# A state scan between projections on one Trainium2 core: a step's small matmuls in two bunches, its transfers merged, Tm copied behind R

## The chip, the cores and the metric

One core of a Trainium2 chip runs the whole program. The metric is the device time of one execution in microseconds; of the kernel before three runs are known. A profile shows one execution. TensorE (PE) multiplies matrices and adds up in PSUM; VectorE (DVE) and ScalarE (ACT) work on tiles in SBUF and PSUM; GpSimd (POOL) does little here; SyncE (SP) issues all transfers from one queue, in order. Every engine works through its own instructions in order.

## The reference, cut to what matters

Two sequences of 512 tokens and 1024 channels (s = 0 and 1) go through two layers. Layer 0 is RWKV-7 time mixing in both directions, 16 heads of 64 channels; its scan is

```
S_t = S_{t-1} (diag(decay_t) + a_t b_t^T) + v_t k_t^T ;  y_t = S_t r_t
```

with r, k, v and a gate z from 1024 x 1024 projections of the shifted input, a group norm behind it, and an output projection w_o. Layer 1 is attention over a neighbourhood of 8 x 16 grid cells, with one input projection (q, k, v, z) and one output projection. All is float32 at the interface; the projections run as three passes of a rounded form (high by high, high by low, low by high).

## The kernel before, in words

The kernel has three stages. A prelude (to about 165 us) norms the inputs and computes z and k of s = 0. The scan phase (about 167 to 1146 us, the last step ends there) is the stage that the change touches. The rest is attention and the remaining projections.

The scan is cut into chunks of 64 tokens. `self.todo` lists 8 pairs (s, pb), each of four heads, and each pair has 8 steps (chunks; both directions are in one step), so there are 64 steps q. For a pair `prep` computes the factors of the chunks and stores them (dram `ab`), `gram` their products, and `inverse` inverts a triangular matrix by 30 elimination steps on VectorE (the tiles N and etmp) and 32 x 32 matmuls. The result is MT. `finish` norms the outputs of a pair.

A step works so, by the names of the code:

- `fetch` loads `cab` (the chunk's factors, two transfers, one per direction) and `V` (four transfers); `fetch_x` loads the other half of `X` (two transfers) from the same dram tile `vt`.
- `near` (L979): 8 matmuls A K^T into a spare part of the bank `zy` of the step before, then VectorE masks them into `AK`.
- `outer` (L1000): 32 matmuls into the tile `pf` (one buffer, shared with `gram`); VectorE masks the first half into `R` (L1024), ScalarE copies the second half into `Tm` (L1031).
- `step` (L1035): `S` times `cab` and `V` times `AK` into `zy` (L1061, L1067); ScalarE copies `Z` (L1073); the solve, MT times Z, into `us` (L1083); ScalarE copies its halves into `X` (L1087); the next state, X times Tm, into `us` (L1093); then the outputs, X times R, into `zy` (L1098); VectorE makes `WS` and `S` (L1107, L1108) and the outputs are copied or added into `y` (L1113, L1115).

Next to it `flow` runs the projections: `loads` brings raw weights, `splits` makes the high half `whi` on ScalarE (L687) and the low half `wlo` on VectorE (L689), `operands` does the same with a column group's inputs (loaded into `xr`, two buffers; copied to `act` at L710 and L712), `products` issues three passes for each of 8 blocks k of a column (L727 to L729), and `posts` runs `column`, which takes the finished column out of its bank `pm`.

What sets the order: in the scan phase the order on TensorE, VectorE and ScalarE is written out by a planner at build time, `weave`. Each of the functions above is a thread; it yields the engine that its next piece needs, a condition (`gate`) and an estimate of when its data is there. `weave` keeps a model clock per engine, and takes, of the threads that are open and ready, the one of the lowest rank, those of TensorE last. Thus `step` (rank 0) goes before `near` (0.5), `outer` (1), `operands` (3.5) and `products` (9), and products fill what is left. `room` and `left` of `Clock` estimate when a bank or buffer is free. On the chip each engine keeps the order that was planned, and waits where a semaphore is late. Outside the scan phase the framework's scheduler sets the order.

In `step` each `yield` is a point at which other work can come between:

```
1089         yield "P", lambda: did["R"] > q and did["X"] > q, lambda c: c.at(name(st.X, st.R[0], *([] if st.last else st.Tm[:1])))
...
1094             yield "P"
```

Of the kernel before, what the change touches and what calls it, by code (L numbers as in the profile page):

```python
# [10 lines left out]
F32 = mybir.dt.float32  # L11
# [38 lines left out]
class Clock:  # L50
# [7 lines left out]
    def __init__(self, nc):  # L58
        self.nc = nc
        self.t = dict.fromkeys("PADGS", 0.0)  # L60
        self.made, self.used = {}, {}
        self.slots = {}
        self.slot = {}
        self.dq = 0.0
        self.mode, self.tiles = None, {}
        self.seen = 0
# [146 lines left out]
class Trunk:  # L213
    NACT, NW, NRAW, NTMP, WP = 18, 4, 3, 5, 512
# [18 lines left out]
    NZ1, STOCK, EPS = 0, 1, 60.0  # L233
# [338 lines left out]
    def shifted(self, s, j):  # L572
        xn, xx = self.shift[s]

        def source(k):
            t = self.t("xr", bufs=2)
# [5 lines left out]
    def reload(self, kind, s):  # L582
        return self.operands(lambda k: self.load(self.t("xr", bufs=2), self.sp[kind, s, k]))


    def column(self, s, kind, p, ps):
# [3 lines left out]
        first = lambda e: (e, None, lambda c, n=ps.tensor.name: c.at([n]))  # L590
        if kind == "z":
# [6 lines left out]
            yield "A" if s == 0 else first("A")  # L598
            act.activation(th, ps, AF.Tanh, scale=0.5)
            yield "D"  # L600
            vt.scalar_tensor_tensor(o, th, 1.0, ps, op0=ALU.add, op1=ALU.mult)
# [3 lines left out]
        o = self.tmp()  # L605
        act.copy(o, ps)
# [4 lines left out]
        if kind == "k":  # L611
            yield "A"
            sq = self.tmp()
# [25 lines left out]
        if p == 0:  # L639
            sp["vt", s] = self.dram(f"vt{s}", (NCH, 4, 2, L, 2, P))  # L640
# [3 lines left out]
        for d in range(2):  # L644
# [8 lines left out]
            for j in range(2):  # L653
                self.load(sp["vt", s][j::2, p // 2, d, :, p % 2].rearrange("m t c -> t m c"), vs[64 * j:64 * j + 64])
# [10 lines left out]
    def flow(self):  # L665
# [5 lines left out]
        raw, w, x = {}, {}, {}  # L671
# [20 lines left out]

        def operands():
            for g, (ready, source, _) in enumerate(self.groups):
                if g == 0:
                    continue
                todo = []
                for k in range(KT + 1):
                    if k < KT:
                        yield "S", lambda: ready() and 8 * g + k < did["x"] + self.NACT // 2 + 1  # L700
                        todo.append(source(k))
                    if k == 0:
                        continue
                    src, before = todo.pop(0)
                    for n, f in enumerate(before):
                        yield "D", None, lambda c: c.at(name(src))
                        f()
                    yield "A", lambda: 8 * g + k - 1 < did["x"] + self.NACT // 2, lambda c: c.at(name(src))
# [4 lines left out]
                    x[g, k - 1] = hi, lo  # L713
# [21 lines left out]
        def posts(a):  # L735
# [7 lines left out]
            Thread(lambda: 0, loads()), Thread(lambda: 3 if few() else 9, splits()), Thread(lambda: 3.5, operands()),  # L743
# [215 lines left out]
    def fetch(self, st):  # L959
# [6 lines left out]
        for d in range(2):  # L966
            self.load(st.ab[:, d].rearrange("p g a t -> p g (a t)"), sp["ab", s, pb][i][:, d])
        for d in range(2):
            for h in range(2):
                self.load(st.V[half(h), d], sp["vt", s][i, pb, d][:, :, 64 * h:64 * h + 64])  # L970

    def fetch_x(self, st):
        sp, s, pb, i, e = self.sp, st.s, st.pb, st.i, st.e
        half = lambda h: slice(64 * h, 64 * h + 64)
        st.X = self.t("X", (P, 2, 2, 2, HD), self.NX, F32, self.front)
        for d in range(2):
            self.load(st.X[half(1 - e[d]), d].rearrange("p g h v -> p (g h v)"), sp["vt", s][i, pb, d].rearrange("t g c -> t (g c)"))

    def near(self, q):  # L979
# [3 lines left out]
        free, room = self.bank()  # L983
        yield (
            "P", lambda: self.did["fetch"] > q and (self.did["solve"] >= q if q else free()),
# [774 lines left out]
```

## Time and profile before

| what | us |
|---|---|
| median of 3 runs | 1789.09 |
| lowest and highest run | 1788.36, 1797.47 |
| the profiled execution | 1786.57 |
| its span, first to last instruction | 1784.6 |
| TensorE busy | 1602.6 (90%) |
| VectorE busy | 1238.0 (69%) |
| ScalarE busy | 978.6 (55%) |
| mean granted clock of TensorE | 0.962 |

The page's shares are over the whole span. The stages differ: behind the scan phase TensorE is always busy, in it it is not. In a row of a timeline the first number is the start, the second the duration, and a bracket at the end is the idle time of the engine before it, with what ended it. The granted clock is a share of 2.4 GHz: 1.0 is that, 0.5 is 1.2 GHz, and a value between is a mixture over the stretch. Matmuls overlap: two that follow each other start closer together than one lasts.

### The profile page before, as it was taken

The numbers are of one execution on the slowest core, as the hardware profiler recorded it, in microseconds if no ns is written. First come the engines' busy times: TensorE is split into PE (matmuls) and PEld (weight loads), VectorE is DVE, ScalarE is ACT, GpSimd is POOL, SyncE is SP. The second block draws the span as 40 slices with busy tenths as digits, with TensorE's granted clock in tenths as the row PEclk, the third lists the DMA queues.
The fourth block names the chain that finished last, engine by engine and source line by source line (L and its number), as shares of the span: only waits on it lengthen the run. The fifth ranks groups of instructions, "written<-read, shape, count | busy, mean of one in ns | idle before, by whom it ended". The sixth has DMA issues, their size and how long they took to land.

```text
span 1784.6 us, 49663 instructions
## 1 busy us (share of the span) xinstructions
PE 1602.6 (90%) x20416; PEld 1231.1 (69%) x20416; DVE 1238.0 (69%) x2693; ACT 978.6 (55%) x1964; POOL 24.2 (1%) x94
## 2 busy tenths in 40 slices
PE   7997767889889888798898977999999999999998
PEld 6775546666556666676675766788777788777776
DVE  8977578877878778886787966532556676655564
ACT  5454456667484575666557443333556665545562
POOL 0000000000000000000000000000000000000000
PEclk9999888999999999999998989999999999999999
DMA  5435667577666577767765775564546346644452
GB/s 197 160 130 199 201 222 220 179 224 212 199 195 204 185 228 219 239 197 228 215 198 187 239 218 159 158 236 149 171 159 198 105 135 219 207 158 148 166 183 95
DMA packets 252675, 336.49 MB, mean 189 GB/s; under 512 B 57280, under 2 KB 122944, under 8 KB 252448
## 3 DMA queue, kind: packets, MB, share of 16 engines
q1 hardware_dynamic: 252448, 333.32, 58.1%
q8 instruction: 160, 2.62, 0.6%
q14 instruction: 67, 0.55, 0.1%
HBM read 227.71 MB, written 105.51 MB: 187 GB/s over the span
## 4 chain that ended last, share of the span: by engine, by line
PE 58%; DVE 18%; DMA 10%; ACT 7%; issue 5%; SPq 1%; DVEq 0%; ACTq 0%
PE pg L403 6%; PE pg L404 6%; PE pg L405 6%; PE pm L727 5%; PE pm L728 4%; PE pm L729 4%; DMA cab<-dab 3%; PE pm L1316 3%; DVE etmp L917 2%; PE po L1344 2%; DVE N L918 2%; PE pt L1331 2%; DVE ab L840 2%; PE pf L1016 2%; SPq L308 1%
## 5 line engine op out<-in xcount | busy, mean ns | idle before, releaser
L727 PE MATMUL pm<-act,whi 128*128 128x512 f32 x608 | 271.5, 447 | 33.7 <-ACT whi L687 18.3
L729 PE MATMUL pm<-act,wlo 128*128 128x512 f32 x608 | 247.2, 407 | 6.4 <-DVE wlo L689 6.3
L728 PE MATMUL pm<-act,whi 128*128 128x512 f32 x608 | 248.0, 408 | 5.5 <-DVE act L712 5.4
L403 PE MATMUL pg<-act,whi 128*128 128x512 f32 x448 | 182.1, 408 | 0.2 <-DVE tmp L1274 0.2
L404 PE MATMUL pg<-act,whi 128*128 128x512 f32 x448 | 178.2, 398 | 0.0
L405 PE MATMUL pg<-act,wlo 128*128 128x512 f32 x448 | 177.8, 397 | 0.0
L353 DVE TENSOR_TENSOR wlo<-raw,whi 128x512 fp32r<-128x512 f32 x156 | 107.1, 688 | 91.5 <-ACT whi L352 76.0
L727 PEld LDWEIGHTS pm<-act,whi 128*128 128x128 f32 x608 | 118.4, 195 | 71.3 <-ACT whi L687 20.4
L352 ACT CAST whi<-raw 128x512 fp32r<-128x512 f32 x156 | 96.3, 618 | 126.2 <-PE pg L404 61.6
L689 DVE TENSOR_TENSOR wlo<-raw,whi 128x512 fp32r<-128x512 f32 x152 | 103.7, 686 | 74.6 <-ACT whi L687 74.4
L729 PEld LDWEIGHTS pm<-act,wlo 128*128 128x128 f32 x608 | 119.3, 196 | 36.7 <-DVE wlo L689 10.5
L728 PEld LDWEIGHTS pm<-act,whi 128*128 128x128 f32 x608 | 119.5, 197 | 31.8 <-DVE act L712 9.4
L687 ACT CAST whi<-raw 128x512 fp32r<-128x512 f32 x152 | 93.8, 620 | 66.2 <-PE pm L728 50.8
L403 PEld LDWEIGHTS pg<-act,whi 128*128 128x128 f32 x448 | 84.4, 188 | 25.5 <-issue 10.4
L405 PEld LDWEIGHTS pg<-act,wlo 128*128 128x128 f32 x448 | 84.3, 188 | 17.9 <-issue 1.7
L404 PEld LDWEIGHTS pg<-act,whi 128*128 128x128 f32 x448 | 84.4, 188 | 17.5 <-issue 2.7
L918 DVE TENSOR_TENSOR N<-etmp,N 128x30 f32<-128x30 f32 (+14 forms) x240 | 79.8, 332 | 8.2
L1327 ACT ACTIVATE sb<-sb,mx 128x256 f32<-128x256 f32 x128 | 64.1, 503 | 36.6 <-DVE mx L1326 36.1
L1031 ACT COPY Tm<-pf 128x512 f32<-128x512 f32 x56 | 32.8, 586 | 92.2 <-DVE R L1024 92.0
L917 DVE TENSOR_TENSOR etmp<-N 128x30 f32<-128x30 f32 (+14 forms) x240 | 78.7, 328 | 5.0
L1016 PE MATMUL pf<-cab 64*64 64x64 f32 x2048 | 51.1, 234 | 29.7 <-DMA cab<-dab 21.4
L1324 DVE CUSTOM_DVE_ANT_0 sb<-pm,bias 128x256 f32<-128x256 f32 x128 | 50.0, 420 | 39.2 <-PE pm L1316 30.2
(370 smaller groups left out, 3424.2 us busy)
## 6 DMA issues: line engine op xcount, KB each, us to landing
dab<-ab SPq DMA_DIRECT2D x32, 1024.0 KB
cab<-dab SPq DMA_DIRECT2D x128, 256.0 KB
raw<-in_w_in_dram SPq DMA_DIRECT2D x128, 256.0 KB
bias<-in_rpb_dram SPq DMA_DIRECT2D x32, 384.0 KB
raw<-in_w_z_dram SPq DMA_DIRECT2D x32, 256.0 KB
dz<-tmp SPq DMA_DIRECT2D x32, 256.0 KB
raw<-in_w_k_dram SPq DMA_DIRECT2D x32, 256.0 KB
dk<-tmp SPq DMA_DIRECT2D x32, 256.0 KB
```

Source lines behind the costliest of these rows:

```text
L352: self.nc.scalar.copy(hi, src)
L353: (eng or self.nc.vector).tensor_tensor(lo, src, hi.bitcast(F32), op=ALU.subtract)
L403: nc.tensor.matmul(ps, hi, x[k][0], start=(k == 0), stop=False)
L404: nc.tensor.matmul(ps, hi, x[k][1], start=False, stop=False)
L405: nc.tensor.matmul(ps, lo, x[k][0], start=False, stop=(k == KT - 1))
L687: nc.scalar.copy(hi, raw[h])
L689: nc.vector.tensor_tensor(lo, raw.pop(h), hi.bitcast(F32), op=ALU.subtract)
L727: nc.tensor.matmul(ps, hi[:, at], xh, start=(k == 0), stop=False)
L728: nc.tensor.matmul(ps, hi[:, at], xl, start=False, stop=False)
L729: nc.tensor.matmul(ps, lo[:, at], xh, start=False, stop=(k == KT - 1))
L917: vt.tensor_tensor(tv, N[:, q + 1:, q:q + 1].broadcast_to([P, n, q]), N[:, q:q + 1, :q].broadcast_to([P, n, q]), op=ALU.mult)
L918: vt.tensor_tensor(N[:, q + 1:, :q], tv, N[:, q + 1:, :q], op=ALU.add)
```

## The change

It does seven things.

1. `near` and `outer` lose their matmuls. A new function `factors(q + 1)` issues both, 8 and 32, directly behind the solve of step q in the same piece of TensorE's order. The solve is issued only when `factors` can be (next `cab` loaded, `pf` free) or when the next step starts a pair. `alone` issues `factors` where no solve before did.
2. Next state and outputs are one piece: the `yield "P"` between them goes. It may be planned 400 ns (`NEAR`) before its inputs are there.
3. `Tm` is copied when `R` is made, by the planner's estimate, and not before step q - 1 is through (`did["steps"] >= q`).
4. `vt` is laid out so that `V` is one transfer, `X` still two; its store has rows of 256 bytes instead of 512. `cab` is one transfer.
5. `xr` has three buffers (`NXR`). A thread `fetched` of rank 0 loads operands; `operands` has rank 2.5.
6. Banks that a column of k or z, or the outer products, will read a second time are noted in `keep`, so that the planner does not count them as free.
7. The index order of `X` and `us` is (h, g) instead of (g, h).

```diff
     def left(self, name):
-        return max(self.used.get(name, {}).values(), default=0.0) if name in self.slot else 1e12
+        return max(self.used.get(name, {}).values(), default=0.0) if name in self.slot and name not in self.keep else 1e12
...
         if p == 0:
-            sp["vt", s] = self.dram(f"vt{s}", (NCH, 4, 2, L, 2, P))
+            sp["vt", s] = self.dram(f"vt{s}", (4, 2, NCH // 2, 2, L, 2, 2, HD))
...
+        def fetched():
+            for g, (ready, source, _) in enumerate(self.groups):
+                for k in range(KT if g else 0):
+                    yield "S", lambda: ready() and 8 * g + k < did["x"] + self.NACT // 2 + self.NXR - 1
+                    todo[g, k] = source(k)
...
-        for d in range(2):
-            self.load(st.ab[:, d].rearrange("p g a t -> p g (a t)"), sp["ab", s, pb][i][:, d])
-        for d in range(2):
-            for h in range(2):
-                self.load(st.V[half(h), d], sp["vt", s][i, pb, d][:, :, 64 * h:64 * h + 64])
+        self.load(st.ab.rearrange("p d g a t -> p (d g a t)"), sp["ab", s, pb][i].rearrange("p d g a -> p (d g a)"))
+        self.load(st.V.rearrange("p d g c -> p (d g c)"), sp["vt", s][pb, i % 2, i // 2].rearrange("h t d g c -> (h t) (d g c)"))
...
+    def factors(self, q):
...
+        st.ak = self.steps[q - 1].room if q else self.p("pm", (P, 2, 2, L))
         for g in range(2):
             for dd in range(2):
                 for h in range(2):
                     nc.tensor.matmul(
-                        ak[half(h), dd, g], ab[half(h), dd, g, 1 + e[dd]], ab[half(h), dd, g, 2 - e[dd]], start=not q, stop=True,
+                        st.ak[half(h), dd, g], ab[half(h), dd, g, 1 + e[dd]], ab[half(h), dd, g, 2 - e[dd]], start=not q, stop=True,
                         skip_group_check=True)
...
+        self.clock.keep.add(st.f.tensor.name)
+        self.did["factors"] += 1
...
-            yield "A", None, lambda c: c.at([f.tensor.name])
+            yield "A", lambda: did["steps"] >= q, lambda c: c.at([R.tensor.name])
...
-        yield "P", lambda: did["inverse"] > st.n and free2(), lambda c: max(c.at(name(Z, self.formed[key][1])), room2(c))
+        near, wide = self.bank("pf")
+        go = lambda: q + 1 < len(self.steps) and did["factors"] == q + 1 and did["fetch"] > q + 1 and near()
+        yield (
+            "P", lambda: did["inverse"] > st.n and free2() and (go() or not self.soon(q + 1)),
+            lambda c: max(c.at(name(Z, self.formed[key][1])), room2(c), max(c.at(name(self.steps[q + 1].ab)), wide(c)) if go() else 0.0))
...
         did["solve"] += 1
+        if go():
+            self.factors(q + 1)
...
-        yield "P", lambda: did["R"] > q and did["X"] > q, lambda c: c.at(name(st.X, st.R[0], *([] if st.last else st.Tm[:1])))
+        yield (
+            "P", lambda: did["R"] > q and did["X"] > q,
+            lambda c: c.at(name(st.X, st.R[0], *([] if st.last else st.Tm[:1]))) - self.NEAR)
...
-            yield "P"
```

Three places show what the planner makes of it. On TensorE, one step in the middle of the phase, before (X is what ScalarE copied from the solve, h and w2h belong to `prep`):

```order
L1061 MATMUL zy_10762<-S_10745,cab_10018 64x64 x16
L1067 MATMUL zy_10762<-V_10019,AK_10701 64x64 x8
L1016 MATMUL pf_10799<-cab_10274 64x64 x16
L1016 MATMUL pf_10799<-cc,cab_10274 64x64 x16
L1083 MATMUL us_10838<-Z_10832,MT_439_1696 64x64 x8
L993 MATMUL zy_10762<-cab_10274 64x64 x8
L796 MATMUL pm_10860<-h_1407_7574,w2h_10663 128x512
L797 MATMUL pm_10860<-h_1407_7574,w2l_10662 128x512
L1093 MATMUL us_10838<-X_10224,Tm_10238 64x64 x8
L796 MATMUL pm_10880<-h_1430_7767,w2h_10663 128x512
L797 MATMUL pm_10880<-h_1430_7767,w2l_10662 128x512
L1098 MATMUL zy_10762<-X_10224,R_10236 64x64 x8
```

and of the changed kernel, a step near it (L1105 is the solve, L1119 the next state, L1123 the outputs):

```order
L1105 MATMUL us_10710<-Z_10702,MT_439_1696 64x64 x8
L998 MATMUL zy_10659<-cab_10187 64x64 x8
L1008 MATMUL pf_10727<-cab_10187 64x64 x16
L1008 MATMUL pf_10727<-cc,cab_10187 64x64 x16
L736 MATMUL pm_10455<-act_8519,whi_10461 128x512
L737 MATMUL pm_10455<-act_8518,whi_10461 128x512
L738 MATMUL pm_10455<-act_8519,wlo_10462 128x512
L1119 MATMUL us_10710<-X_10293,Tm_10688 64x64 x8
L1123 MATMUL zy_10659<-X_10293,R_10656 64x64 x8
L736 MATMUL pm_10455<-act_8533,whi_10461 128x512
L737 MATMUL pm_10455<-act_8532,whi_10461 128x512
L738 MATMUL pm_10455<-act_8533,wlo_10462 128x512
```

The outer products moved from before the solve to behind it, and the outputs moved up to the next state. On ScalarE, around the copies of a step, before:

```order
L1073 COPY Z_10989<-zy_10911 128x256
L1031 COPY Tm_11000<-pf_10956 128x512
L652 COPY vs_11012<-pm_10993 128x512
L1087 COPY X_10758<-us_11002 64x256 x2
L852 ACTIVATE pp_11033<-th_1924_10897,dv 128x512
L652 COPY vs_11040<-pm_11027 128x512
```

and of the changed kernel:

```order
L1111 COPY X_10908<-us_10998 64x256 x2
L809 ACTIVATE th_1979_11090<-pm_11063,dv 128x512
L813 ACTIVATE u_11092<-th_1979_11090,ones 128x512
L1138 COPY y_10177<-zy_10957 128x256
L1048 COPY Tm_11104<-pf_11015 128x512
L809 ACTIVATE th_1988_11140<-pm_11094,dv 128x512
L660 COPY vs_11142<-pm_11099 128x512
L1091 COPY Z_11181<-zy_11108 128x256
```

Tm stood between Z and X of a step; now it stands behind X and y, and ahead of the next step's Z. On VectorE, around the update of a state, before (ab, kp belong to `prep`, etmp and N to `inverse`):

```order
L1024 TENSOR_TENSOR R_10998<-pf_10956,mrx_1693 128x512
L840 TENSOR_TENSOR ab_10953<-pp_10954,u_10950 128x4x2x64
L997 TENSOR_TENSOR AK_11016<-zy_10911,cc 128x256
L917 TENSOR_TENSOR etmp_10651<-N_10649 128x210
L918 TENSOR_TENSOR N_10649<-etmp_10651,N_10649 128x10x21
L689 TENSOR_TENSOR wlo_10688<-raw_10481,whi_10687 128x512
L855 TENSOR_TENSOR kp_1946_11055<-pp_11033,k_10656 128x512
L840 TENSOR_TENSOR ab_10953<-kp_1946_11055,u_10950 128x4x2x64
L1107 TENSOR_TENSOR WS_11074<-us_11002,S_10893 128x256
L1108 TENSOR_TENSOR S_11073<-WS_11074,wc_7484 128x256
```

and of the changed kernel:

```order
L1031 TENSOR_TENSOR AK_11051<-zy_10957,cc 128x256
L864 TENSOR_TENSOR kp_1973_11055<-pp_11053,k_10627 128x512
L849 TENSOR_TENSOR ab_10931<-kp_1973_11055,u_10928 128x4x2x64
L1041 TENSOR_TENSOR R_11068<-pf_11015,mrx_1693 128x512
L1132 TENSOR_TENSOR WS_11087<-us_10998,S_10949 128x256
L1133 TENSOR_TENSOR S_11086<-WS_11087,wc_7020 128x256
L1188 TENSOR_TENSOR bv_10695<-pm_10919,bv_10695 128x512
```

The work of the other threads that stood between R and WS moved ahead of R or behind S.

## Rows read from the trace of the kernel before

**Rows 1.** The page's head and its count of transfer packets.

```profile
span 1784.6 us, 49663 instructions
...
DMA packets 252675, 336.49 MB, mean 189 GB/s; under 512 B 57280, under 2 KB 122944, under 8 KB 252448
```

**Rows 2.** Busy time by stage: PE, PEld, DVE, ACT, POOL, clock, DMA share, GB/s.

```profile
170.00:305.00 135.00, 92.67 (x913) 69.82 (x915) 97.30 (x171) 73.12 (x137) 6.20 (x11) 0.86 0.65 212
305.00:1146.00 841.00, 724.36 (x15594) 552.64 (x15589) 649.06 (x1244) 493.62 (x977) 16.11 (x39) 0.95 0.66 205
1146.00:1785.00 639.00, 630.04 (x3288) 490.45 (x3286) 351.92 (x1018) 329.13 (x711) 0.00 (x0) 1.00 0.50 166
```

**Rows 3.** TensorE's waits, 170 to 1146: total us, times, longest us.

```profile
PE pf L1016 <- DMA cab<-dab: 21.4, 19, 4.2
PE pm L727 <- ACT whi L687: 18.3, 4, 14.3
PE pm L727 <- ACT act L710: 11.4, 5, 7.1
PE us L1083 <- ACT Z L1073: 9.9, 12, 1.7
...
PE pf L1016 <- ACT Tm L1031: 8.2, 3, 3.6
...
PE pm L729 <- DVE wlo L689: 6.3, 8, 1.5
PE us L1093 <- ACT X L1087: 6.1, 7, 2.1
...
PE zy L1061 <- DVE S L1108: 3.9, 4, 2.3
```

**Rows 4.** Timeline of TensorE around one lone next-state group, full clock.

```profile
901.09 0.39 PE L728 MATMUL pm<-act,whi 128*128 128x512 f32 x1
901.32 0.40 PE L729 MATMUL pm<-act,wlo 128*128 128x512 f32 x1
901.65 0.69 PE L1093 MATMUL us<-X,Tm 128*64 128x64 f32 x16
902.26 0.50 PE L796 MATMUL pm<-h,w2h 128*128 128x512 f32 x1
902.60 0.40 PE L797 MATMUL pm<-h,w2l 128*128 128x512 f32 x1
```

**Rows 5.** The same around a solve with A K^T directly behind it.

```profile
851.36 0.40 PE L729 MATMUL pm<-act,wlo 128*128 128x512 f32 x1
851.69 0.68 PE L1083 MATMUL us<-Z,MT 64*64 64x64 f32 x16
852.20 0.63 PE L993 MATMUL zy<-cab 64*64 64x64 f32 x16
852.77 0.50 PE L796 MATMUL pm<-h,w2h 128*128 128x512 f32 x1
```

**Rows 6.** SP's issues of cab and V: ns min/median/max, first and last start.

```profile
L308 SPq DMA_DIRECT2D cab<-dab x128: 319/430/2650, 242.3 to 1127.4; - x128
...
L308 SPq DMA_DIRECT2D V<-dvt x256: 512/597/2153, 291.0 to 1129.8; - x128
```

**Rows 7.** The tiles R, WS, Tm: durations, and ScalarE's idle time before Tm.

```profile
L1024 DVE TENSOR_TENSOR R<-pf,mrx x64: 642/684/693, 300.6 to 1135.1; 128x512 f32<-128x512 f32 x64
...
L1107 DVE TENSOR_TENSOR WS<-us,S x48: 386/418/446, 342.7 to 1138.9; 128x256 f32<-128x256 f32 x48
...
  DVE R L1024: 92.0, 45
```

**Rows 8.** ScalarE's timeline at the start of the scan phase.

```profile
183.14 0.62 ACT L710 CAST act<-xr 128x512 fp32r<-128x512 f32 x1 [5.23 <-DMA xr<-dlv]
183.66 1.13 ACT L687 CAST whi<-raw 128x512 fp32r<-128x512 f32 x2
```

**Rows 9.** VectorE's waits, 305 to 1146: total us, times, longest us.

```profile
DVE R L1024 <- PE pf L1016: 33.4, 17, 4.8
...
DVE WS L1107 <- PE us L1093: 5.3, 7, 1.4
```

More of the change, by code (lines that the diff above doesn't have):

```diff
@@ L590, in column @@
         first = lambda e: (e, None, lambda c, n=ps.tensor.name: c.at([n]))
+        keep, whole = self.clock.keep, ps.tensor.name
         if kind == "z":
@@ L691, in splits @@
                 did["split"] += 1
-        def operands():
[L694 to L705, printed above, removed]
+        def fetched():
[3 more added lines that the diff above has]
+                    todo[g, k] = source(k)
+        def operands():
+            for g in range(1, len(self.groups)):
+                for k in range(KT):
+                    yield "S", lambda: (g, k) in todo
+                    src, before = todo.pop((g, k))
+                    for f in before:
                         yield "D", None, lambda c: c.at(name(src))
                         f()
-                    yield "A", lambda: 8 * g + k - 1 < did["x"] + self.NACT // 2, lambda c: c.at(name(src))
+                    yield "A", lambda: 8 * g + k < did["x"] + self.NACT // 2, lambda c: c.at(name(src))
                     lo, hi = self.pair()
@@ L976, in fetch_x @@
         for d in range(2):
[L977 to L979 removed]
+            self.load(
+                st.X[half(1 - e[d]), d].rearrange("t h g c -> t h (g c)"),
+                sp["vt", s][pb, i % 2, i // 2, :, :, d].rearrange("h t g c -> t h (g c)"))
+    def factors(self, q):
         nc, st = self.nc, self.steps[q]
         half = lambda h: slice(64 * h, 64 * h + 64)
[L983 to L986 removed]
         ab, e = st.ab, st.e
[L988 to L989 removed]
+        st.ak = self.steps[q - 1].room if q else self.p("pm", (P, 2, 2, L))
         for g in range(2):
@@ new lines, in alone, with near @@
+    def alone(self, q):
+        did, st = self.did, self.steps[q]
+        free, room = self.bank("pf")
+        bank, here = self.bank()
+        yield (
+            "P", lambda: did["factors"] > q or (did["fetch"] > q and (did["solve"] >= q if q else bank()) and free()),
+            lambda c: 0.0 if did["factors"] > q else max(c.at([st.ab.tensor.name]), room(c), 0.0 if q else here(c)))
+        if did["factors"] == q:
+            self.factors(q)
+    def near(self, q):
+        nc, did, st = self.nc, self.did, self.steps[q]
+        yield "D", lambda: did["factors"] > q, lambda c: c.at([st.ak.tensor.name])
+        st.AK = self.t("AK", (P, 2, 2, L), self.NAK, F32, self.front)
+        nc.vector.tensor_tensor(st.AK, st.ak, self.mstrict.unsqueeze(1).unsqueeze(1).broadcast_to([P, 2, 2, L]), op=ALU.mult)
+        did["AK"] += 1
@@ L1027, in outer @@
         st.R = [R[:, :, d] for d in range(2)]
         if not st.last:
-            yield "A", None, lambda c: c.at([f.tensor.name])
+            yield "A", lambda: did["steps"] >= q, lambda c: c.at([R.tensor.name])
             Tm = self.t("Tm", (P, 2, 2, 2, L), self.NTM, F32, self.front)
-            self.after(nc.scalar.copy(flat(Tm), flat(f[:, :, 1])), ends[1:])
+            self.after(nc.scalar.copy(flat(Tm), flat(st.f[:, :, 1])), st.ends[1:])
             st.Tm = [Tm[:, :, d] for d in range(2)]
-        self.did["R"] += 1
+        self.clock.keep.discard(st.f.tensor.name)
@@ L1035, in step @@
+        did["R"] += 1
     def step(self, q):
@@ L1116, in step, with soon @@
         did["steps"] += 1
+    def soon(self, q):
+        return q < len(self.steps) and self.did["factors"] == q and self.steps[q].i > 0
     def finish(self, s, pb, y):
```

74 lines of the change are left out of this document (36 added, 38 removed).

## The prediction

> **What bounds the kernel now.** I read the page's head first, then busy time by stage, then TensorE's waits in the stage that has any. The profiled execution took 1786.57 us, 2.0 more than its span [rows 1], and the median of the three runs is 2.5 us above it. So sums are made against 1786.6, and 2.5 is added at the end. By stage [rows 2]: from 1146 us on TensorE is busy in 630 of 639 us at full clock, and nothing there can be gained by waiting less. From 305 to 1146, where the 64 steps of the state scan run between products of the projections, it is busy 724 of 841 us, at a mean clock of 0.95. Since the clock has only two levels, 2.4 and 1.2 GHz, 0.95 means 10% of the stretch, some 84 us, at 1.2 GHz. From 170 to 305 it is busy 93 of 135 us at 0.86. There is always product work left for TensorE (it runs on for 100 us after the last step), so the end is set by TensorE's own work plus what it idles and what it loses in changing tile shapes before 1146. The waits name the idle time [rows 3]: 21.4 us for cab (a step's operands), 18.3 for a weight half, 14.3 of it once, 11.4 for operands of a new column group, 24.2 together for Z, Tm and X, which ScalarE copies out of PSUM, and only 3.9 for the state S. VectorE is the next engine, 649 of 841 us [rows 2].
>
> **Part 1, bunching on TensorE.** Two products start 0.23 us apart. A lone group of 16 small matmuls between two products moves the next product to 0.94 us and the one behind it to 0.34 instead of 0.23, so it costs 0.82 us [rows 4]. With a second group of 16 directly behind the first the next product comes at 1.41 instead of 0.94 [rows 5]: the second costs 0.47, and 0.35 us is what standing alone costs. Counted over the order of TensorE from the scan's first product to the last step, the shape of the tiles changes 524 times before and 475 times after, 49 fewer: next state and outputs stood apart nearly everywhere, and the 16 + 32 matmuls of A K^T and the outer products now follow the solve. 49 x 0.35 = 17 us less. All of it is TensorE's own time, where it does not fall into a wait. Ends: -10, if some fall there, and -19, since at 1.2 GHz each costs double.
>
> **Part 2, transfers.** A step's V comes in one transfer instead of four, cab in one instead of two; X stays at two. An issue of V takes SP 0.60 us and one of cab 0.43 (medians) [rows 6], so SP has 3 x 0.60 + 0.43 = 2.2 us less per step, in order, ahead of the next cab. The outer products, which did the waiting for cab, also move behind the solve, later in the step. Ends: all 21.4 us go, or none do. I take -13, because the longest single wait was 4.2 us, and two issues' worth of queue covers the usual one of 1 us but not that. Packets do not get fewer: V goes from 32,768 of 256 B to 8,192 of 1 KB, X from 8,192 of 1 KB to 16,384 of 512 B, and the store of vt from 16,384 of 512 B to 32,768 of 256 B. The page counts 57,280 under 512 B [rows 1]: the 32,768 of V and some 16 for the completion of each of about 1,540 transfers. With 256 transfers fewer that count should come to about 53,200. A rule speaks against the new store: the Trainium skill, "DMA: Bandwidth & Descriptors" (Specifications), wants at least 512 B per transfer for line rate, since smaller ones are read, modified and written. No row here prices a packet of 256 B alone. By that rule part 2 would give nothing, the sum below would be 13 us higher, and it is a rival.
>
> **Part 3, ScalarE's order.** Tm is read from the bank that VectorE reads for R, and ScalarE sat 92.0 us in 45 of 56 copies until R was done [rows 7]. X or Z often stood right behind it on ScalarE, and TensorE behind those: 9.9 + 8.2 + 6.1 = 24.2 us [rows 3]. Now a step's X and its outputs go first, then Tm, whose R came right after the solve, then Z. That takes the long ones away, though not the bare handover of a copy: I take -9, ends -20 and 0. Tm is wanted a whole step later, so its own delay is hidden.
>
> **Part 4, operands.** A third xr buffer and a thread of its own let loads run one tile further ahead. The start of the scan loses 14.3 us because the second weight half stands on ScalarE behind an operand that waited 5.23 us for its load [rows 8]; in the new order this load stands ahead of the three stores and the load that it followed in SP's queue. The waits at the next group were 11.4 us [rows 3]. I take -11 of 25.7, ends -20 and 0.
>
> **Part 5, what VectorE pays.** In the new order 37 of 48 updates WS stand directly behind R, with nothing between; before it was 3. R starts when the first half of the outer products is out, about 1.5 us after the solve began (three groups of 0.5 us [rows 5]), and takes 0.68 us [rows 7], so it ends at 2.2. The matmul WS waits for comes behind the rest of the bunch (2.0 us), one product in three passes (0.9) and its own 0.6 [rows 4]: 3.5 to 3.6. VectorE thus stands about 1.4 us per step before WS, 37 x 1.4 = 52 us. Today it waits there 5.3 us in all [rows 9]. Queued behind the waiting WS are the low halves of weights and operands and the elimination, and TensorE's products wait for those. VectorE has 841 - 649 = 192 us free, some of it already spent in waits as for R, 33.4 us [rows 9]. So the ends are 0 and +52. I take +22, under half, because WS, S and then the next step come sooner in exchange.
>
> **Part 6, at no cost or nearly.** The planner's new notes on banks that have a second reader change no instruction. The solve is now issued only when the next step's cab and the pf bank are there; products fill that time on TensorE (the cover), and if it were gone a wait for pf would cost what Tm cost, 8.2 us in 3 waits [rows 3], so 1 to 4 us each. The clock: 84 us at half speed lose at most 42, and with less waiting I take -4, ends -15 and +5.
>
> **Sum.** -17 - 13 - 9 - 11 + 22 - 4 = -32: 1786.6 - 32 = 1754.6, and 1757 beside a median. All the good ends together give -19 - 21 - 20 - 20 - 15 = -95, all the bad ones -10 + 5 + 52 = +47; neither is likely whole.
>
> **Rivals.** (a) VectorE becomes the bound, and it is slower than before. Place: the update WS at the head of VectorE's queue. If none of the 52 us is absorbed, the copies and operands that gave parts 2 and 3 come late anyway, and the sum is -17 - 11 + 52 = +24, so 1813. It decides when VectorE's busy time and waits fill the stretch. For it: 77% busy, and its waits stand in order. Against: today TensorE waits only 6.3 us for a weight's low half and 3.9 for S [rows 3].
> (b) The state becomes the wait, and nothing changes. Behind the next-state matmuls stood two products of three passes (0.9 each) and the outputs (0.6) before S was wanted, 2.4 us [rows 4]; now 0.5 of outputs and one such product remain, 1.4 us. WS and S take 0.42 us each [rows 7] and a handover, some 0.95 in all, so 0.45 us is spare. If VectorE comes a microsecond late on average, 56 steps x 0.55 = 31 us eat the gain: 1788.
> (c) The waits go entirely: -17 - 21 - 20 - 20 - 8 + 15 = -71, so 1718. For it: nearly all of these waits are queue order, and queue order is what changes.
> (d) The transfers stay late, as packets of 256 B take the queue's time: 1757 + 13 = 1770. Beside it stands the rule of the Trainium skill named in part 2.
> That the bunches are not formed can be left out: the order shows them in 51 of 64 solves.
>
> **How the numbers follow.** The forecast 0.43, with (d) 0.12 beside it; its own range is 1738 to 1778. (c) 0.18, (b) 0.14, (a) 0.13. The range runs from 1718, within (c), to 1798, short of (a): about 0.09 is left out at either end. A measurement of this kernel tells about 0.5% from no change, 9 us. Faster by more than that, below 1780: 0.43 + 0.12 + 0.18 = 0.73. Within it, (b): 0.14. Slower, (a): 0.13.
>
> **What would show it.** The stretch of the steps is TensorE's: its waits for cab should fall below 10 us, those for Z, Tm and X to 15, and ScalarE's 92 us for R nearly vanish. A bunch of solve, A K^T and outer products should read about 2.2 us. VectorE's wait for the next-state matmuls should rise from 5 us to about 50. If TensorE's waits for S and for low halves rise by more than 30 us together, part 5 was too small. If waits for cab stay at 20, part 2 was wrong. Packets under 512 B should come to about 53,200. The time behind the scan should not change; if it does, the forecast rests on the wrong stage.

## The result and the profile after

The changed kernel took 1761.76 us (median of four runs, 1761.46 to 1768.63), beside 1789.42 for the kernel before on the same chip: a ratio of 0.9845 [0.9808, 0.9882]. That is 28 us less where 32 were forecast, 5 us above the predicted time and inside its range. The total is near; what follows shows that several of its terms were not, and that their errors cancelled. One of the ten runs of a kernel below, that of the merged transfers, took 2574 us at a granted clock of 0.65, and its ratio leaves that run out.

The head of the page after, with TensorE's busy time and the packets (before, [rows 1]: span 1784.6, 57280 packets under 512 B; TensorE was busy 1602.6 us):

```profile
span 1759.7 us, 49418 instructions
...
PE 1605.0 (91%) x20416; PEld 1229.6 (70%) x20416; DVE 1239.2 (70%) x2693; ACT 980.2 (56%) x1966; POOL 24.3 (1%) x94
...
DMA packets 240385, 336.46 MB, mean 191 GB/s; under 512 B 53184, under 2 KB 118848, under 8 KB 240160
```

Busy time by stage after, columns as in [rows 2]; the last step now ends at 1119 and no longer at 1146:

```profile
170.00:305.00 135.00, 102.48 (x917) 76.36 (x917) 100.80 (x175) 78.44 (x149) 6.31 (x11) 0.91 0.72 232
305.00:1119.00 814.00, 721.21 (x15612) 548.82 (x15612) 647.45 (x1243) 489.88 (x970) 16.11 (x39) 0.92 0.67 210
1119.00:1760.00 641.00, 628.57 (x3268) 488.86 (x3268) 351.79 (x1016) 330.51 (x711) 0.00 (x0) 0.99 0.51 164
```

Behind the scan nothing changed (641 us against 639). The gain lies in the 841 us that became 814. Beside [rows 2] two things stand out: TensorE's busy time there is nearly what it was, and the clock fell from 0.95 to 0.92, so some 130 us of the stretch (814 x 0.08 x 2) ran at 1.2 GHz, where before it was 84. The second is a comparison of two single executions, and the one before is not a usual one: its mean clock over the whole span is 0.962, while 54 other runs of that kernel, made with the experiments, lie between 0.946 and 0.963, at 0.953 in the mean. The eight runs of the changed kernel have 0.952 in the mean.

TensorE's waits after, 170 to 1146 (total us, times, longest), beside [rows 3]:

```profile
PE pm L737 <- DVE act L721: 12.5, 11, 3.4
PE pm L1194 <- DVE y L1179: 11.3, 3, 7.9
PE pm L736 <- ACT act L719: 8.8, 5, 2.8
PE pm L736 <- ACT whi L697: 8.2, 3, 5.5
PE pm L738 <- DVE wlo L699: 6.6, 7, 2.4
...
PE us L1119 <- ACT X L1111: 4.2, 6, 1.3
...
PE zy L1079 <- DVE S L1133: 2.1, 3, 0.7
...
PE zy L998 <- DMA cab<-dab: 1.5, 2, 1.2
...
PE us L1105 <- ACT Z L1091: 1.2, 3, 0.6
```

The wait for cab is gone (21.4 to 1.5), so is that for Tm, Z is at 1.2 and X at 4.2, and the start of the scan waits 5.5 us for its weight half instead of 14.3. New at the top stand waits for VectorE: the low half of an operand (act L721) and y of the finish (L1179). The rows of the kernel before for these two:

```profile
PE pm L728 <- DVE act L712: 5.4, 7, 1.6
...
PE pm L1165 <- DVE y L1150: 0.6, 1, 0.6
```

With all rows of this view added up by the engine that ended the wait, the account of TensorE's waits reads:

| ended by | before | after | difference | forecast |
|---|---|---|---|---|
| DMA | 23.8 | 1.5 | -22.3 | -13 (part 2) |
| ScalarE | 69.7 | 52.3 | -17.4 | -20 (parts 3 and 4) |
| VectorE | 39.5 | 56.7 | +17.2 | +22 (part 5) |
| issue | 24.5 | 17.3 | -7.2 | none |
| sum | 157.5 | 127.8 | -29.7 | -11 |

VectorE's own waits, 305 to 1120 after:

```profile
DVE AK L1031 <- PE zy L998: 50.1, 41, 4.7
DVE wlo L699 <- ACT whi L697: 33.6, 17, 6.3
DVE WS L1132 <- PE us L1119: 12.3, 22, 3.1
```

and the row of the kernel before for AK, which [rows 9] did not need:

```profile
DVE AK L997 <- PE zy L993: 26.4, 24, 2.3
```

The wait for R, 33.4 us in [rows 9], fell out of the longest; it is this row of the same view:

```profile
DVE R L1041 <- PE pf L1008: 2.3, 5, 0.7
```

That for AK took its place (26.4 to 50.1), and that for WS rose from 5.3 to 12.3 and not to 50.

ScalarE's copy Tm, and what its engine waited for ahead of it, beside the 92.0 us of [rows 7]:

```profile
L1048 ACT COPY Tm<-pf x56: 572/590/646, 288.7 to 1106.6; 128x512 f32<-128x512 f32 x56
...
  DVE R L1041: 31.7, 18
```

One step on TensorE at full clock, with the bunch and then next state and outputs together (start, us, engine, line, operation, tiles):

```profile
845.42 0.39 PE L738 MATMUL pm<-act,wlo 128*128 128x512 f32 x1
845.74 0.68 PE L1105 MATMUL us<-Z,MT 64*64 64x64 f32 x16
846.25 0.57 PE L998 MATMUL zy<-cab 64*64 64x64 f32 x13
...
847.18 0.64 PE L1008 MATMUL pf<-cc,cab 64*64 64x64 f32 x30
847.75 0.50 PE L736 MATMUL pm<-act,whi 128*128 128x512 f32 x1
...
848.65 0.69 PE L1119 MATMUL us<-X,Tm 128*64 128x64 f32 x16
849.16 0.64 PE L1123 MATMUL zy<-X,R 128*64 128x64 f32 x16
849.73 0.50 PE L736 MATMUL pm<-act,whi 128*128 128x512 f32 x1
...
850.62 0.69 PE L1079 MATMUL zy<-S,cab 64*64 64x64 f32 x32
```

The bunch takes 2.01 us from its first matmul to the next product. The state came back in time here: 1.97 us from the next-state matmuls (848.65) to the matmuls that read S (850.62).

**Where the 25 us of the two spans lie.** TensorE's time was split in three: outside its busy time (span less busy), busy time lost to the low clock (half of the busy time that the records of the clock put at 1.2 GHz, an estimate), and the rest, its work at full clock.

| kernel | span | outside busy | lost to the clock | work |
|---|---|---|---|---|
| before | 1784.6 | 182.0 | 53.2 | 1549.4 |
| changed | 1759.7 | 154.7 | 66.9 | 1538.1 |
| changed, again | 1754.5 | 156.5 | 56.4 | 1541.6 |
| outputs apart (below) | 1743.8 | 140.8 | 48.5 | 1554.5 |

So the change brought 25 to 27 us less idle time and 8 to 11 us less work and, against this one profile of before, paid 3 to 14 us of it back at the low clock. By the mean clock of all runs (0.953 and 0.952) the last part is about nothing. That of the outputs apart, 0.966 in four runs, does differ.

### The profile page after: what moved, and what is told of

The parts are those of the page before. It is cut to its first block, busy times and chain, and to the rows that moved or that the text cites. A ratio compares the mean times of both kernels' runs of the same rounds, so it can differ in the third digit from the quotient of the medians.

```text
span 1759.7 us, 49418 instructions
## 1 busy us (share of the span) xinstructions
PE 1605.0 (91%) x20416; PEld 1229.6 (70%) x20416; DVE 1239.2 (70%) x2693; ACT 980.2 (56%) x1966; POOL 24.3 (1%) x94
## 2 busy tenths in 40 slices
DMA packets 240385, 336.46 MB, mean 191 GB/s; under 512 B 53184, under 2 KB 118848, under 8 KB 240160
## 4 chain that ended last, share of the span: by engine, by line
PE 67%; DVE 14%; DMA 7%; ACT 7%; issue 4%; SPq 1%; DVEq 0%; ACTq 0%
PE pm L736 6%; PE pg L404 6%; PE pg L405 6%; PE pg L406 6%; PE pm L737 5%; PE pm L738 5%; PE pm L1345 3%; PE pf L1008 2%; PE po L1373 2%; PE pt L1360 2%; PE us L1105 2%; PE zy L1079 2%; DVE etmp L926 2%; PE us L1119 1%; PE zy L404 1%
## 5 line engine op out<-in xcount | busy, mean ns | idle before, releaser
L736 PE MATMUL pm<-act,whi 128*128 128x512 f32 x608 | 275.2, 453 | 24.7 <-ACT act L719 8.8
L737 PE MATMUL pm<-act,whi 128*128 128x512 f32 x608 | 251.7, 414 | 12.8 <-DVE act L721 12.5
L736 PEld LDWEIGHTS pm<-act,whi 128*128 128x128 f32 x608 | 120.6, 198 | 65.5 <-ACT act L719 11.2
L737 PEld LDWEIGHTS pm<-act,whi 128*128 128x128 f32 x608 | 121.5, 200 | 40.2 <-DVE act L721 19.2
L738 PEld LDWEIGHTS pm<-act,wlo 128*128 128x128 f32 x608 | 121.0, 199 | 38.0 <-DVE wlo L699 11.3
L404 PEld LDWEIGHTS pg<-act,whi 128*128 128x128 f32 x448 | 84.3, 188 | 23.8 <-issue 9.1
L1031 DVE TENSOR_TENSOR AK<-zy,cc 128x256 f32<-128x256 f32 x63 | 26.6, 422 | 50.3 <-PE zy L998 50.1
L1111 ACT COPY X<-us 64x256 f32<-64x256 f32 x128 | 46.9, 366 | 25.1 <-PE us L1105 22.8
```

Source lines behind the costliest of these rows:

```text
L404: nc.tensor.matmul(ps, hi, x[k][0], start=(k == 0), stop=False)
L736: nc.tensor.matmul(ps, hi[:, at], xh, start=(k == 0), stop=False)
L737: nc.tensor.matmul(ps, hi[:, at], xl, start=False, stop=False)
L738: nc.tensor.matmul(ps, lo[:, at], xh, start=False, stop=(k == KT - 1))
```

## The experiments

They come in three groups: parts of the change laid one at a time on the kernel before, parts taken out of the changed kernel, and a load put on VectorE. Each ratio is against the kernel before, run between the others on the same chip.

### The keep notes alone

The first four kernels share the planner's notes on banks with a second reader; this one has nothing else.

```diff
+        self.keep = set()
...
-        return max(self.used.get(name, {}).values(), default=0.0) if name in self.slot else 1e12
+        return max(self.used.get(name, {}).values(), default=0.0) if name in self.slot and name not in self.keep else 1e12
...
+        self.clock.keep.add(f.tensor.name)
...
+        self.clock.keep.discard(f.tensor.name)
```

> The kernel before with the notes on banks that are read a second time (part 6 alone). The forecast has it at no cost: 0 us against the kernel before, within 4 either way. Rival: the notes themselves move the planned order enough to matter, and then 10 us or more, either way.

Measured: 1803.68 us, 1.0051 [1.0029, 1.0073]. About 9 us slower, so the expectation of nothing was a miss. The notes add no instruction, but they change what the planner counts as free, and with it the order: the last step ends at 1160 us instead of 1146, and outside its busy time TensorE has 187.6 us instead of 182.0. The clock does not carry it: 0.952 in the mean of the runs, as for the kernel before on the same chip. It is the base for the next three.

### The merged transfers

```diff
-        for d in range(2):
-            self.load(st.ab[:, d].rearrange("p g a t -> p g (a t)"), sp["ab", s, pb][i][:, d])
-        for d in range(2):
-            for h in range(2):
-                self.load(st.V[half(h), d], sp["vt", s][i, pb, d][:, :, 64 * h:64 * h + 64])
+        self.load(st.ab.rearrange("p d g a t -> p (d g a t)"), sp["ab", s, pb][i].rearrange("p d g a -> p (d g a)"))
+        self.load(st.V.rearrange("p d g c -> p (d g c)"), sp["vt", s][pb, i % 2, i // 2].rearrange("h t d g c -> (h t) (d g c)"))
```

with the layout of vt and the order of X and u that go with it, on top of the notes.

> The kernel before with the notes on banks and the merged transfers of V and cab with the new layout of vt (part 2). Part by part (the forecast): TensorE's wait for cab falls from 21 us to about 8 and the time by 13 against keep_alone. Rival, place and not transfers: the outer products still stand before the solve as early as they did, so the wait for cab stays at 15 or more and the time within 5 us.

Measured: 1790.32 us, 0.9970 [0.9949, 0.9991], which is 13 us below the notes alone: the time is as expected. TensorE's wait for cab, 170 to 1146, in the notes alone and then here:

```profile
PE pf L1023 <- DMA cab<-dab: 20.2, 21, 2.9
```

```profile
PE pf L1025 <- DMA cab<-dab: 12.2, 6, 4.6
```

The many short waits are gone and six long ones stay. The row stands between the two readings (8 and 15 us), and its 8 us are the part of the 13 that the waits show. That the merging alone does it is not shown either: the next kernel, with the transfers as before, has this row at 9.8 us, and the one with the factors apart and Tm early (below), with the transfers merged, has

```profile
PE pf L1025 <- DMA cab<-dab: 26.7, 12, 4.5
```

Where the outer products stand in the bunch, the wait is 7.6 us in one piece with Tm early and 1.5 in the whole change. What removes it there is their new place.

### The operands' own thread and third buffer

```diff
+    NXR = 3
...
+        def fetched():
+            for g, (ready, source, _) in enumerate(self.groups):
+                for k in range(KT if g else 0):
+                    yield "S", lambda: ready() and 8 * g + k < did["x"] + self.NACT // 2 + self.NXR - 1
+                    todo[g, k] = source(k)
...
-            Thread(lambda: 3.5, operands()),
+            Thread(lambda: 0, fetched()), Thread(lambda: 2.5, operands()),
```

> The kernel before with the notes on banks, the third xr buffer and the loading thread (part 4). Part by part: 11 us less than keep_alone, the wait of 14 us at the start of the scan phase down to 6. Rival: the waits come back elsewhere, since more loads stand ahead of the weights in SP's queue, and the time stays within 4 us.

Measured: 1791.32 us, 0.9976 [0.9952, 1.0001], 12 us below the notes alone: as expected. TensorE's wait for the weight half, in the notes alone and then here:

```profile
PE pm L734 <- ACT whi L694: 15.3, 2, 13.0
```

```profile
PE pm L733 <- ACT whi L694: 7.7, 2, 5.3
```

The longest wait, at the start of the scan, goes from 13.0 to 5.3 us. That is the step the prediction named for it, and 8 of the 12 us.

### Tm's late place alone

```diff
-            yield "A", None, lambda c: c.at([f.tensor.name])
+            yield "A", lambda: self.did["steps"] >= q, lambda c: c.at([R.tensor.name])
```

> The kernel before with the notes on banks and Tm planned behind R and behind the step before (part 3). Part by part: 9 us less than keep_alone, ScalarE's 92 us of waiting for R down to 30 or less. Rival: Tm comes so late that the next state waits for it, and the time is the same or up to 10 us more.

Measured: 1922.54 us, 1.0725 [1.0676, 1.0773]: 119 us slower than the notes alone, where 9 less were expected. TensorE's waits, 170 to 1300:

```profile
PE pm L734 <- ACT act L717: 34.0, 16, 6.6
PE pm L953 <- DVE NA L932: 23.9, 3, 14.4
...
PE zy L1000 <- DMA cab<-dab: 20.3, 4, 13.1
PE pf L1023 <- ACT Tm L1039: 20.2, 7, 8.2
```

There is one pf bank. The next step's outer products need it back, and Tm, copied late, holds it. The wait named so is 20 us; that the rest stands behind it, in the planned order and in all queues, is a reading at this point. By the split above, against the notes alone, it is 96 us more outside busy time and 49 us more lost at the low clock (0.911 in the mean of the runs), less 15 of work. The outcome said either that part 3 was wrong altogether, or that Tm's late place belongs to the bunch. Two kernels of the next group decide it.

### The changed kernel again

No edit; it is the base for those that take a part out of the change.

> The changed kernel once more. If its long stretches at half clock (about 130 us of the steps' stretch against 84 before) belong to the kernel, they come again within 15 us. If they are chance of the one execution, they differ by 25 us or more and the span with them.

Measured: 1756.52 us (1752.44 to 1769.40), 0.9805 [0.9759, 0.9852]. The gain is 28 to 34 us. By the clock's records 111 us of the steps' stretch stood at 1.2 GHz (131 in the first profile, 84 before). The two differ by 20 us, which is neither of the two readings. What settles it is the mean clock of all runs, 0.953 before and 0.952 here: the changed kernel's low stretches are its usual ones, and those of the profile before were short for that kernel.

### Next state and outputs apart again

```diff
                     nc.tensor.matmul(so[half(h), d, g], st.Tm[d][:, h, g], st.X[:, d, h, g], start=True, stop=True)
+            yield "P"
```

> The changed kernel with the point between next state and outputs put back, so that other work can come between. Theory of tile shapes: about 45 more lone groups at 0.35 us each, 16 us more. Rival (b) turned round: with the outputs apart the state has more cover, and the time is the same or less. On the clock: if bunches of small matmuls hold the clock down, the share at half clock falls here.

Measured: 1741.91 us, 0.9713 [0.9683, 0.9744]: 15 us faster than the changed kernel and 2.9% below before. By the price of shapes alone it should have been slower. Busy time by stage, and VectorE's longest waits, 305 to 1134:

```profile
170.00:305.00 135.00, 106.61 (x911) 79.79 (x909) 101.27 (x173) 76.68 (x144) 6.16 (x11) 0.86 0.70 226
305.00:1134.00 829.00, 744.61 (x15737) 561.76 (x15738) 653.39 (x1254) 498.31 (x987) 16.12 (x39) 0.95 0.66 212
1134.00:1744.00 610.00, 598.63 (x3148) 464.71 (x3148) 344.15 (x1005) 319.50 (x695) 0.00 (x0) 1.00 0.50 166
```

```profile
DVE AK L1031 <- PE zy L998: 45.8, 37, 4.9
DVE wlo L699 <- ACT whi L697: 28.4, 21, 3.2
```

Counted over the whole trace, the shape changes 770 times here, 88 more than in the changed kernel (682; before 732). At 0.35 us for the two changes of a lone group that is 15 us more work, and the table above has 13 to 16 more. So the price read from [rows 4, 5] holds. But idle time falls by 14 to 16 us and the loss at the low clock by 8 to 18, and these outweigh it. The mean clock is 0.966 in the four runs, above that of the changed kernel and of the one before. The last step even ends later (1134 against 1119), with more products done by then: only 610 us remain behind it.

### The outer products and A K^T apart again

The functions and threads of the kernel before for A K^T and the outer products, in an otherwise changed kernel (Tm stays late):

```diff
-        if go():
-            self.factors(q + 1)
...
-            Thread(lambda: 0, each(self.step)), Thread(lambda: 0.5, each(self.alone)), Thread(lambda: 0.5, each(self.near)),
+            Thread(lambda: 0, each(self.step)), Thread(lambda: 0.5, each(self.near)),
```

> The changed kernel with A K^T and the outer products issued apart again, by the threads of the kernel before, outside the solve. Theory of tile shapes alone: a few more lone groups, 0.35 us each, so 2 to 6 us more. Theory of place: the outer products go early again and wait for cab, and Tm for R, so 10 to 20 us more.

Measured: 1898.77 us, 1.0587 [1.0542, 1.0633]: 142 us slower than the changed kernel, far from either theory. VectorE's waits, 305 to 1360:

```profile
DVE R L1034 <- PE pf L1025: 72.0, 50, 3.8
DVE WS L1119 <- PE us L1106: 60.3, 46, 5.1
```

Again the late Tm, as the next kernels show: the outer products come only when it has left the bank, and R and the update behind R stand.

### Tm early, with the bunch and without

```diff
-            yield "A", lambda: did["steps"] >= q, lambda c: c.at([R.tensor.name])
+            yield "A", None, lambda c: c.at([st.f.tensor.name])
```

once in the changed kernel:

> The changed kernel with Tm planned as before: as soon as the outer products are there, whether R is or not. Theory (part 3 has its worth inside the bunches): ScalarE waits for R again, some 60 to 90 us, and the time goes up by 5 to 15 against the changed kernel. Rival: with the bunches Tm's place matters little, since R follows the solve at once, and the time is within 5 us.

and once in the kernel with the factors apart:

> factors_apart, with Tm planned as before. Two readings of the 142 us that factors_apart cost: if it is Tm's late copy that holds the one pf bank and so keeps outer products and grams out, nearly all of it goes here, to within 30 us of the changed kernel. If it is the bunch itself that is worth so much, most of the 142 us stays.

Measured: 1767.34 us, 0.9870 [0.9833, 0.9907], and 1797.53 us, 1.0038 [1.0015, 1.0061]. The four together, in us:

| | Tm late | Tm early |
|---|---|---|
| A K^T and outer products apart | 1898.8 | 1797.5 |
| in the bunch | 1756.5 to 1761.8 | 1767.3 |

Of the 142 us, 101 are Tm's late place without the bunch. With it the late place is worth some 5 to 11 us, and with the intervals as they are (0.9870 against 0.9845 and 0.9805) it may be next to nothing. The bunch itself is worth 30 us where Tm is early, on one chip. ScalarE's idle time before Tm, apart and early:

```profile
  DVE R L1034: 101.7, 48
```

The 92 us of [rows 7] are back there, and TensorE's waits for X and Z with them (10.9 and 5.8 us). In the bunch with Tm early ScalarE waits even longer,

```profile
  DVE R L1041: 117.1, 55
```

and TensorE still has only 1.7 and 6.9 us for X and Z. So it is the bunch, more than Tm's late place, that keeps ScalarE's wait from reaching TensorE.

The bunch's 30 us are not a matter of shapes: with Tm early the shape changes 662 times with it and 627 without, 35 more, since the kernel before had the outer products directly ahead of the solve. They are mostly waits (25 us of it lie outside TensorE's busy time). TensorE's waits, 170 to 1146, fall from 162.6 us to 133.2: by DMA from 30.6 to 12.4, by ScalarE from 73.1 to 52.1, by its own issue from 26.6 to 18.1, while those by VectorE rise from 32.4 to 50.5. That is the pattern of the whole change.

### More work for VectorE

Behind each update of the state the sum is written twice more, to no use: 96 instructions of 424 ns, 40.7 us.

```diff
                 vt.tensor_tensor(st.S, sm, wc, op=ALU.mult)
+                for _ in range(2):
+                    vt.tensor_tensor(sm, so, before.S, op=ALU.add)
```

In the changed kernel:

> The changed kernel with two more passes of WS, without use, behind each of 48 updates: 48 x 2 x 0.42 = 40 us more work on VectorE in the steps' stretch. If VectorE is the bound there, 30 to 40 us more. If it has slack, as the forecast has it with under half of its waiting reaching TensorE, 5 to 18 us more.

and with the outputs apart:

> outputs_apart with the same 40 us of useless work on VectorE that cost the changed kernel 33. If putting the outputs apart frees VectorE (it no longer stands before WS), it costs less here, 5 to 20 us. If VectorE is as much the bound as there, 30 to 40.

Measured: 1789.85 us, 0.9981 [0.9959, 1.0003], and 1777.68 us, 0.9934 [0.9894, 0.9974]. The 40.7 us cost 33 and 36. VectorE is therefore close to a bound in both, at 79 and 80% busy in the stretch. By the split above TensorE has about 20 us more outside its busy time (156.5 to 176.0, and 140.8 to 163.4) and loses about 20 more at the low clock (0.953 to 0.942 and 0.966 to 0.950 in the mean of the runs), with 10 us less work. TensorE's waits in the first, 170 to 1146:

```profile
PE pm L955 <- DVE NA L934: 18.7, 1, 18.7
PE zy L1079 <- DVE y L1142: 11.3, 7, 2.0
...
PE pm L738 <- DVE wlo L699: 9.9, 8, 3.4
```

That the outputs apart are faster because they free VectorE, my reading until then, falls with the second number: the same load costs as much there.

### Outputs apart with Tm early

Both edits, `yield "P"` and Tm by its own bank.

> outputs_apart with Tm planned as before. If Tm's place is worth 5 to 15 us inside the bunches, it is that much slower than outputs_apart. If it is worth nothing there, within 5 us of it.

Measured: 1740.98 us (1734.33 to 1745.34), 0.9720 [0.9678, 0.9763], the same as with Tm late. Where the outputs stand apart Tm's place is worth nothing. Either is about 1% faster than the changed kernel and 2.8% faster than before.

**The parts in one line.** As changes of the ratio: notes +0.5%, transfers -0.8%, operands -0.75%, which would make 0.9896 if they add. The factors apart with Tm early, which have these three and next state and outputs joined, stand at 1.0038, so the joining, with the 400 ns of `NEAR`, costs 1.4%. Taken directly, with Tm early and on one chip, it costs 26 us (1767.3 against 1741.0), or 1.5%; with Tm late 15 us. The bunch behind the solve brings 1.7% (1797.5 to 1767.3), and Tm's late place at most 0.65%.

## Why the prediction came out, step by step

**Part 1, bunching (-17; measured -8 to -11 of work).** The price was right, the count was not. I multiplied 49 changes of shape by 0.35 us, but 0.35 is what a lone group costs, and a lone group makes two changes, one into its shape and one out of it. 49 / 2 x 0.35 = 8.6, inside what was measured; the 88 changes of outputs apart give the same price. The Trainium skill, "TensorEngine Tiling (Array Packing)" (Key Properties), says that a change of tiling mode drains TensorE; the price of about 0.17 us per change in these runs fits that, though no row shows a drain as such. The second error is what the count was credited to: the fewer changes all come from joining next state and outputs (88 and, with Tm early, 113), while the bunch behind the solve adds some (35 with Tm early). And by the ladder of runs the two bunches have opposite signs, both against their shapes: that of the solve is worth 30 us and that of the outputs costs 15 to 26.

**Part 2, transfers (-13; measured -13 alone, -22 of waits in the whole).** Alone it gave the forecast number, of which 8 us are the wait for cab; that SP's queue is the mechanism is not shown. Mis-sized was what the new place of the outer products adds: I kept the long waits as not covered by two issues, and the place covers them. In the whole change it is the place that counts, since with the transfers merged and the old place cab was waited for 26.7 us. Packets under 512 B came to 53,184 (forecast about 53,200). Rival (d), that the 256 B store takes the gain away, falls: 13 us were gained with that store. The rule behind it, of at least 512 B for line rate (the Trainium skill, "DMA: Bandwidth & Descriptors", Specifications), is not tested by that: in the changed kernel TensorE waited 1.5 us for transfers in all, and for none from vt. SP's issue of V also became shorter, 382 ns against the 597 of [rows 6]:

```profile
L309 SPq DMA_DIRECT2D V<-dvt x64: 319/382/1442, 284.2 to 1104.3; - x64
```

**Part 3, ScalarE's order (-9 of 24.2; measured -19).** Z, Tm and X stand at 5.4 us (forecast 15), and ScalarE's 92.0 us at 31.7. But it is no part by itself. With the bunch and Tm early Z, Tm and X stand at 8.6 us already, so most of the 19 is the bunch's. "Its own delay is hidden" is the sentence that failed: Tm's delay holds the one pf bank, and it is hidden only because the bunch asks for that bank behind the next solve. Alone it cost 119 us.

**Part 4, operands (-11; measured -12 alone).** Right in size, and in place at the start: 14.3 to 5.5 us. At the next groups nothing was gained in the whole change: the wait for an operand's high half fell from 11.4 to 8.8 us, that for its low half rose from 5.4 to 12.5.

**Part 5, VectorE before WS (+22; measured +17, in another place).** TensorE's waits that VectorE ended rose by 17 us, near the forecast. But the wait for the next-state matmuls, forecast at 50 us, is 12.3, and S and the low halves of weights, 11 us before with the state's other branch, are 9. The step that failed is the 1.4 us of standing per step, and in it the early R. In the trace after, 36 of the 48 updates WS stand directly behind R, and the next state ends 3.6 us after its solve began (medians here and below): both as forecast. But R starts at 2.8 us, not at 1.5, and ends at 3.5, since AK stands ahead of it on VectorE and waits for the bunch first, and two more instructions stand between AK and R. That leaves 0.2 us of standing before WS. VectorE's waits for R, WS and AK together came to 65 us before (33.4 + 5.3 + 26.4) and 65 after (2.3 + 12.3 + 50.1): they moved, and did not grow. The 17 us that TensorE pays are in two rows, the operands' low halves (5.4 to 12.5) and y of the finish (0.6 to 11.3, of which one wait is 7.9). That they come from VectorE's standing before AK, or before a weight half of ScalarE's (9.8 us before, 33.6 after), is likely and not shown. The total came near by luck. That VectorE has no 192 us free to give, as part 5 feared, the extra load confirms: 33 of 40.7 us came through.

**Part 6, the notes and the clock (0 and -4; measured +9 alone, and about 0).** "The notes change no instruction" is true and not the point: they change the order. For the clock I argued that less waiting means less time at 1.2 GHz. TensorE did wait less, and the mean granted clock stayed where it was: 0.953 in 54 runs before, 0.952 in 8 after. The profiles alone would say that it got worse: by the clock's records of the steps' stretch, 84 us at 1.2 GHz in 20 falls before, 131 us in 13 after and 111 in 16 in the second profile. But the profile before, from which the term of 84 us was taken, has a higher clock than all but one of the other runs of that kernel. With the outputs apart, 75 us in 13 falls and a mean of 0.966 in four runs, the argument holds.

**The sum.** Waits -30 instead of -11, work -8 to -11 instead of -17, clock +3 to +14 in these profiles instead of -4: -25 to -30 in the spans, beside -32. It came out by offsetting errors of 6 to 19 us, not by its steps. The one that would have misled a tuner is part 1: it credits the joining of next state and outputs with a gain, and that edit is a loss.

**Rivals.** (a), VectorE as the bound and slower than before, did not come, though the added load shows how near it is. (b), the state as the next wait, did not set the time: S was waited for 2.8 us in all. From the next-state matmuls to the next step's matmuls on S the median fell from 3.08 us to 1.39, measured from the end of the one to the start of the other, as forecast (1.4). S was ready 0.39 us (median) before the matmuls that read it, so the margin I put at 0.45 us was there. (c) was nearest for cab and Tm, whose waits went almost wholly (1.5 and 0.3 us are left).

**Still open.** Why next state and outputs apart give less idle time (14 to 16 us, with Tm early 19), and why the clock is lower when they are together (0.952 in both pairs beside 0.966 and 0.967 in the means of the runs). Both are measured, on two pairs of kernels. That VectorE is freer with the outputs apart is ruled out by the load. `NEAR` was not tried alone, nor the index order of X and u, which came with the merged transfers. Whether the clock falls because small matmuls stand together, or because the waits lie otherwise, no run here separates.

## What to carry to other kernels

Price a bunch by what it saves per group, count both edges of a group only once, and then test each joined pair by itself: here the bunch that saved no change of shape was worth 30 us by the waits it took away, and the one that saved 88 changes cost 15. Before a clock seen in one profile goes into a sum, compare it with the clock of the other runs. A copy moved later holds its buffer longer, so ask who wants the buffer next before calling its delay hidden. When a wait's releaser changes, add the waits up by engine, before and after: the totals of ScalarE and VectorE were forecast better here than the places.

## What the runs showed of the hardware

- A group of 16 small matmuls between products of 512 columns costs 0.82 us alone and 0.47 behind another; 88 more changes of shape made 13 to 16 us of TensorE's work at full clock.
- Less idle time did not always come with a higher clock: outside its busy time TensorE had 25 to 27 us less after the change, and the mean granted clock stayed (0.953 in 54 runs, 0.952 in 8). With next state and outputs apart, 14 to 16 us less again, it was 0.966 (4 runs); in the changed kernel with 20 us more, by the load on VectorE, it was 0.942 (10 runs).
- An issue of a transfer on SP got shorter with its shape: V as one piece of 1 KB rows took 382 ns (median), one quarter of it in 256 B rows had taken 597.
